# Three groups of seven products in the second pair of both down stages of a hybrid layer

## The chip, the cores and the metric

The kernel runs on 1 core of one Trainium2 chip. The metric is the device time of one execution in microseconds (us). The kernel before took 1831.77, 1834.62 and 1834.78 us in three runs, a median of 1834.62 us.

## The reference

The reference is one layer on 256 rows of width 2048, in float32. The inner width of each SwiGLU is 5632. Only the lines that bear on the change are shown:

```python
def swiglu(h, w_gate, w_up, w_down):
    return (jax.nn.silu(h @ w_gate) * (h @ w_up)) @ w_down
...
#  x += 1/2 * SwiGLU(RMSNorm(x))                 FFN1
#  h = RMSNorm(x);  [u | q | k | v] = h @ w_in
#  y_ssm = GLU(S5(u)),  y_sb = StickBreakingAttention(QKNorm(q), QKNorm(k), v)
#  x += concat(RMSNorm(y_ssm), RMSNorm(y_sb)) @ w_out
#  x += 1/2 * SwiGLU(RMSNorm(x))                 FFN2
#  x += RMSNorm((p @ w_ple_proj) * sigmoid(RMSNorm(x) @ w_ple_gate))
```

The weights of the two SwiGLU blocks are by far the largest inputs: two times three matrices of 2048 by 5632.

## The kernel before

**Products in three parts.** TensorE (PE) multiplies in a rounded float32 form (fp32r). To keep float32 accuracy every operand is split into a high and a low part: ACT casts the high part (L181), DVE subtracts it from the source for the low part (L184). A product is then three matmuls: high by high (L322, L494), activation low by weight high (L323, L495) and activation high by weight low (L327, L497). Weights arrive as `raw`, 1 MB blocks of 512 rows by 512 columns, by loads on SP's queue (L312 in columns, L511 in groups), with five buffers. Each half of such a block is split into a pair of tiles, `whi` and `wlo`, or `shi` and `slo`; where groups of seven run, `weight_pair` hands out seven such pairs in turn. Activations of a SwiGLU's inner width are split one block of 512 rows at a time (`act`, tiles `hhi` and `hlo`).

**Columns and groups of seven.** In the down stages two neighbouring column blocks of 512 (the two sides, a pair) are computed together, over eleven row blocks of the down weight, numbered 0 to 10. For one row block the program has two ways. `column(side, kb)` is the plain product, for one side: two halves of twelve matmuls, so 48 matmuls for both sides. `chunk(kb)` is a group of seven products for both sides, after Strassen's scheme as Winograd wrote it: 42 matmuls. The group takes its weights from two loads, builds three sums of them on DVE (`sum`, L501) and one by a DMA that adds in place, issued on POOL (`raw<-raw`, L525), and splits all seven operands. It needs sums of the activation's quarters too (`sum_forms`: four small DVE operations on `rows`, L458, and a split into `nhi` and `nlo`). PE takes the products of a group in the order 1, 5, 6, 4, 2, 3, 7.

**The plan of a down stage.** `plans` lists for the first and the second pair of columns what is done in which order: c is a column block for both sides, s a group of seven, a the rest of the blocks. A down stage has two pairs here, since the output has four blocks of 512 columns. `kept` holds the split of one row block, so that both sides of a column share it. After the last group, `opened` gathers finished banks into the residual `x` by seven operations of DVE (L674, L680, L685); it is put off to run beside the work that follows. While the second pair begins, the finished columns of the first pair are turned and fetched back for the next stage: `h<-mid`, small DMAs on SP (L229), and their normed split (`nhi`, `nlo`, L191 and L193).

**FFN2's first block.** The gate and up product of FFN2 goes over eleven blocks of 512 columns of the inner width. For each the program mixes groups and columns, with gate and up as the two sides and the row blocks 0 to 3 of the weight. The first block alone is done by `gemm_pair`, by columns only.

**Other places of the change.** At the start of the projection `w_in` the S5 mixer loads a table in eight pieces (`m<-scr_h`, `load_m3`, L1053, on SP); `u_block` (L1015) casts a finished block of u into `sg`, and `ua<-ub` (L1032, SP) moves it. `add_square` (L1327, L1328) squares a block on ACT into `sqp`, and POOL adds it up.

All engines execute in program order. A waiting instruction holds all that stands behind it on its engine; DMAs that SP issues stand in SP's own queue.

Of the kernel before, what the change touches and what calls it, by code (L numbers as in the profile page):

```python
# [16 lines left out]
P = 128  # L17
# [9 lines left out]
NB = 512  # L27
SL = 4
# [5 lines left out]
def layer_kernel(ctx: ExitStack, tc: tile.TileContext, a: dict, shapes: dict, out: bass.AP):  # L34
    nc = tc.nc
# [307 lines left out]
    def gemm_pair(act, ws, nkt):  # L343


        ps = [[acc(), acc()] for _ in ws]
        last = nkt // 4 - 1
        for ks in (range(last - 1), (last - 1,), (last,)):
            for (w, n0), banks in zip(ws, ps):
                for k in ks:  # L350
                    part = act(k)
                    for half in list(weight_halves(w, 4 * k, 4, n0)):
                        gemm_half(banks, (part, half), range(TT), k + half[0] == 0, k == last and half[0] == 1)
                        step()
                if last in ks:
                    yield banks
# [198 lines left out]
    def ffn(i, xn, nxt, bg=None):  # L555
# [23 lines left out]
        for f in range(NF):  # L579
            if prep and f == early:  # L580
                finish(prep)
                side.close()
                prep = None
                sevens = pools.enter_context(sums_phase(f"sums{i}"))
                hp = pools.enter_context(phase(f"h{i}b"))
                sums = [sum_forms(sevens, whole_rows(sevens, xn(kb)), "h") for kb in range(2)]
            if sevens and f:
                sg, hh = com("sg"), com("h")
                gate_cols, up_cols = ([u[:, t * NB : (t + 1) * NB] for t in range(TT)] for u in (sg, hh))

# [13 lines left out]

                s = Seven(xn, lambda kb: sums[kb], ((wg, f * NB), (wu, f * NB)), sevens)
                two = f != early
                if f == early:
                    s.column(0, (1, 2, 3))
                    s.chunk(0, (*shared, 2, 4))
                    put_off(0, opened, s)  # L610
                elif two:
                    s.chunk(0)
                    s.column(0, (2, 3))
                    s.chunk(1, (*shared, 2, 4))
                    put_off(0, opened, s)
                else:
                    s.chunk(0, shared)
                    put_off(0, opened, s)
                    s.column(0, (1, 2, 3), True)
                put_off(0, gated, s)  # L620
                s.column(1, (2, 3) if two and f != early else (1, 2, 3), True)
                nc.vector.tensor_tensor(out=hh, in0=s.banks[3.8], in1=hh, op=ALU.add)
                for t in range(TT):
                    nc.vector.scalar_tensor_tensor(
                        out=up_cols[t], in0=up_cols[t], scalar=xn.rs(t), in1=gate_cols[t], op0=ALU.mult, op1=ALU.mult
                    )
                put_off(2, turned, hp, f, hh)
                continue

            def gate():  # L630
                for t in range(TT):
# [3 lines left out]
            if f == 0 and bg:  # L635
                warm_up(10)
                first = first_quarters(wg, xn)
            if f == 0 and not bg:
                both = gemm_pair(xn, ((wg, 0), (wu, 0)), KD)
                pg = next(both)  # L640
                sums = [sum_forms(sevens, whole_rows(sevens, xn(kb))) for kb in range(2)]
            else:
                pg = gemm_block(xn, wg, f * NB, KD, first)
            sg = com("sg")
            if f == 0 and bg:
# [6 lines left out]
            pu = gemm_block(xn, wu, f * NB, KD) if f or bg else next(both)  # L652
# [23 lines left out]
        def opened(s, n):  # L676
# [10 lines left out]
            gather(xt[1][n + 1], one, -0.5)  # L687

        plans = (
            ("c3", "c4", "s0", "c5", "c6", "s1", "c7", "c8", "s2", "c9", "c10"),  # L690
            ("c2", "c3", "s0", "c4", "s1", "a5"),
        )
        for n in range(0, ND, 2):
            parts = {}

            def kept(kb):
                if kb not in parts:
                    parts.clear()
                    parts[kb] = act(kb)
                return parts[kb]  # L700
# [7 lines left out]
            s = Seven(kept, lambda kb: sum_forms(sevens, rows(kb)), ((wd, n * NB), (wd, (n + 1) * NB)), sevens)  # L708
            plan = plans[n // 2]
            left = sum(u[0] == "s" for u in plan)  # L710
            for u in plan:
                kb, final = int(u[1:]), u == plan[-1]
                if u[0] == "s":
# [320 lines left out]
    def s5_main(pool, zpool):  # L1034
# [15 lines left out]
        def load_m3(z):  # L1050
            for g in range(2):
                p0 = 64 * g + HC * z
                nc.sync.dma_start(m3[p0 : p0 + HC, :, HC * z :], scr_h[g, :, :, : (SL - z) * HC])  # L1053

# [267 lines left out]
    def add_square(pool, total, src, first):  # L1322
        if first:
            nc.scalar.activation(total, src, AF.Square)
        else:
            sq = get(pool, "sqp", T, 2)
            nc.scalar.activation(sq, src, AF.Square)  # L1327
            nc.gpsimd.tensor_tensor(out=total, in0=total, in1=sq, op=ALU.add)  # L1328

# [345 lines left out]
```

## Time and profile before

| | |
|---|---|
| runs, us | 1831.77, 1834.62, 1834.78; median 1834.62 |
| the profiled execution, us | 1829.94 |
| its span, us | 1828.1 |
| PE busy, matmuls | 1817.1 us (99%), 8960 in the trace |
| DVE busy, instructions | 1523.8 us (83%), 1789 |
| ACT busy, instructions | 1056.1 us (58%), 1228 |
| granted TensorE clock | 1.00 |
| loads of the down weights | 88 of 1024 KB, median 5.2 us from issue to landing |

The span is the part of the profiled execution that the trace covers. Busy time counts an engine's own instructions; a matmul's row (0.39 us) lasts longer than the distance to the next row's start (0.23), so rows of matmuls overlap. A row of a timeline gives the start, the length, the engine, the line, the operation and its tiles; "x4" means four in a row, and the brackets say how long the engine was idle before it and what ended that. FFN1's down stage lies at about 500 to 705 us and its second pair begins near 594.6; FFN2's second pair begins near 1603.

### The profile page before, as it was taken

Reading aid. Unit: us, or ns where it says so; the run is one execution under the profiler, and the core shown is the slowest. Engines: PE = TensorE matmul, PEld = TensorE weight load, DVE = VectorE, ACT = ScalarE, POOL = GpSimd, SP = SyncE. Lnnn points to the kernel's source line nnn. Section 1 sums busy time; section 2 is a strip of 40 time slices with the busy share of each in tenths; the row PEclk is TensorE's granted clock in tenths of the full one; section 3 lists DMA queues with packets and bytes.
Section 4 is the critical chain, followed back from the end, with each engine's and each line's share of the span. In section 5 each row is a group of like instructions: output and inputs, shape, how many; then the busy total and the mean of one; then the engine's idle time right before and its main releaser. Section 6 shows DMA issues by size and latency. Waiting matters only on the chain.

```text
span 1828.1 us, 24219 instructions
## 1 busy us (share of the span) xinstructions
PE 1817.1 (99%) x8960; PEld 1504.4 (82%) x8960; DVE 1523.8 (83%) x1789; ACT 1056.1 (58%) x1228; POOL 96.7 (5%) x147
## 2 busy tenths in 40 slices
PE   9999999999999999999999999999999999999998
PEld 7888888888888888788897888888888888888887
DVE  8966759999899895687566789999999998989565
ACT  7444445556566664455685466555565556666554
POOL 0010000000000000010021000000000010000000
PEclk9999999999999999999999999999999999999999
DMA  9898867787777676675636787887777786767563
GB/s 329 281 290 279 246 224 231 235 248 220 251 244 240 185 253 198 208 254 162 219 134 212 225 301 215 252 256 251 237 225 237 240 273 227 238 206 246 176 217 127
DMA packets 237207, 424.74 MB, mean 232 GB/s; under 512 B 27328, under 2 KB 51264, under 8 KB 236928
## 3 DMA queue, kind: packets, MB, share of 16 engines
q1 hardware_dynamic: 227104, 390.71, 64.2%
q0 software_dynamic: 9264, 31.07, 7.8%
q8 instruction: 70, 1.15, 0.3%
q10 hardware_dynamic: 720, 1.41, 0.2%
q14 instruction: 49, 0.40, 0.1%
HBM read 372.41 MB, written 10.88 MB: 210 GB/s over the span
## 4 chain that ended last, share of the span: by engine, by line
PE 98%; DMA 1%; ACT 1%; DVE 0%; SPq 0%; issue 0%; ACTq 0%; DVEq 0%
PE acc L322 18%; PE acc L323 18%; PE acc L327 18%; PE aux L327 6%; PE aux L323 6%; PE aux L322 6%; PE acc L497 4%; PE acc L495 4%; PE acc L494 4%; PE aux L495 3%; PE aux L494 3%; PE aux L497 3%; PE aux L1135 0%; PE acc L1391 0%; PE acc L1386 0%; PE acc L1382 0%
## 5 line engine op out<-in xcount | busy, mean ns | idle before, releaser
L184 DVE TENSOR_TENSOR wlo<-raw,whi 128x1024 fp32r<-128x1024 f32 x489 | 592.2, 1224 | 179.9 <-ACT whi L181 178.8
L181 ACT CAST whi<-raw 128x1024 fp32r<-128x1024 f32 x489 | 508.1, 1050 | 362.8 <-PE acc L323 227.2
L322 PE MATMUL acc<-whi,nhi 128*128 128x512 f32 x1076 | 421.9, 392 | 4.7 <-ACT whi L181 4.3
L323 PE MATMUL acc<-whi,nlo 128*128 128x512 f32 x1076 | 419.0, 389 | 0.0
L327 PE MATMUL acc<-wlo,nhi 128*128 128x512 f32 x1076 | 294.9, 389 | 0.0
L322 PEld LDWEIGHTS acc<-whi,nhi 128*128 128x128 f32 x1076 | 202.1, 188 | 49.5 <-ACT whi L181 5.9
L327 PEld LDWEIGHTS acc<-wlo,nhi 128*128 128x128 f32 x1076 | 202.0, 188 | 42.1
L323 PEld LDWEIGHTS acc<-whi,nlo 128*128 128x128 f32 x1076 | 202.0, 188 | 41.0
L184 DVE TENSOR_TENSOR slo<-raw,shi 128x1024 fp32r<-128x1024 f32 x177 | 216.1, 1221 | 21.9 <-ACT shi L181 21.5
L181 ACT CAST shi<-raw 128x1024 fp32r<-128x1024 f32 x177 | 185.8, 1050 | 61.0 <-DMA raw<-in_ffn_w_down 26.3
L181 ACT CAST whi<-sum 128x1024 fp32r<-128x1024 f32 x69 | 72.7, 1053 | 137.5 <-DVE sum L501 125.5
L181 ACT CAST shi<-sum 128x1024 fp32r<-128x1024 f32 x48 | 50.6, 1054 | 83.4 <-DVE sum L501 81.3
L501 DVE TENSOR_TENSOR sum<-sum,raw 128x1024 f32<-128x1024 f32 x78 | 95.3, 1222 | 0.5
L184 DVE TENSOR_TENSOR wlo<-sum,whi 128x1024 fp32r<-128x1024 f32 x69 | 84.5, 1224 | 5.7 <-ACT whi L181 4.7
L525 POOL DMA_DIRECT2D raw<-raw x39 | 33.7, 865 | 954.6 <-DVE sum L501 575.2
L184 DVE TENSOR_TENSOR hlo<-hT,hhi 128x1024 fp32r<-128x1024 f32 x56 | 68.3, 1220 | 4.9 <-ACT hhi L181 4.9
L323 PE MATMUL acc<-whi,hlo 128*128 128x512 f32 x184 | 71.9, 391 | 0.1
L322 PE MATMUL acc<-whi,hhi 128*128 128x512 f32 x184 | 71.6, 389 | 0.0
L181 ACT CAST hhi<-hT 128x1024 fp32r<-128x1024 f32 x56 | 58.5, 1046 | 7.3 <-PE aux L327 5.2
L322 PE MATMUL aux<-whi,hhi 128*128 128x512 f32 x160 | 62.2, 389 | 0.0
L323 PE MATMUL aux<-whi,hlo 128*128 128x512 f32 x160 | 62.2, 389 | 0.0
L184 DVE TENSOR_TENSOR slo<-sum,shi 128x1024 fp32r<-128x1024 f32 x48 | 58.7, 1223 | 1.0 <-ACT shi L181 0.7
(373 smaller groups left out, 3164.6 us busy)
## 6 DMA issues: line engine op xcount, KB each, us to landing
raw<-in_ffn_w_up SPq DMA_DIRECT2D x88, 1024.0 KB, 5.6
raw<-in_ffn_w_down SPq DMA_DIRECT2D x88, 1024.0 KB, 5.2
raw<-in_ffn_w_gate SPq DMA_DIRECT2D x86, 1024.0 KB, 7.4
raw<-in_w_in SPq DMA_DIRECT2D x32, 1024.0 KB, 5.9
raw<-raw POOLq DMA_DIRECT2D x39, 512.0 KB, 6.2
raw<-in_w_out SPq DMA_DIRECT2D x16, 1024.0 KB, 5.1
raw<-in_w_ple_gate SPq DMA_DIRECT2D x16, 1024.0 KB, 5.3
hT<-mid SPq DMA_DIRECT2D x160, 64.0 KB, 4.1
```

Of the source, the lines that this page charges most:

```text
L181: copy = nc.scalar.copy(hi, src)
L184: nc.vector.tensor_tensor(out=lo, in0=src, in1=hi.bitcast(F32), op=ALU.subtract)
L322: nc.tensor.matmul(ps[t], lhsT=lh, rhs=hi[:, j, cols], start=start and j == 0, stop=False)
L323: nc.tensor.matmul(ps[t], lhsT=ll, rhs=hi[:, j, cols], start=False, stop=False)
L327: nc.tensor.matmul(ps[t], lhsT=lh, rhs=lo[:, j, cols], start=False, stop=stop and j == 1)
L494: nc.tensor.matmul(ps, lhsT=lh[j], rhs=hi[:, j], start=begin and j == 0, stop=False)
L495: nc.tensor.matmul(ps, lhsT=ll[j], rhs=hi[:, j], start=False, stop=False)
L497: nc.tensor.matmul(ps, lhsT=lh[j], rhs=lo[:, j], start=False, stop=z in final and j == 1)
L501: nc.vector.tensor_tensor(out=t, in0=x, in1=y, op=ALU.add)
L525: nc.gpsimd.dma_start(b12, b22, accum_op=ALU.add)
```

## The change

It has four parts. The second pair of both down stages has a new plan: c10 and c9, then the groups of blocks 2, 1 and 0 one after the other, then columns 3 to 8, where the second side runs them backwards. `kept` now keeps two splits, and across the two pairs, so that blocks 9 and 10 (split last by the first pair) and block 8 at the turn of the sides are not split again; `summed` keeps the rows' sums of blocks 1 and 2 for the second pair. The first block of FFN2 gets one group of seven, for row block 0. The eight pieces of the S5 table are loaded through POOL's queue. `sqp` has six buffers instead of two.

```diff
@@ ffn: gate and up @@
-            if sevens and f:
+            if sevens:
...
-                two = f != early
-                if f == early:
+                if f == 0:
+                    sums = [sum_forms(sevens, whole_rows(sevens, xn(0)))]
+                    s.column(0, (1,))
+                    s.column(1, (1,))
+                    s.chunk(0, shared)
+                    put_off(0, opened, s)
+                    s.column(0, (2,))
+                    s.column(1, (2,))
+                    s.column(0, (3,), True)
+                    sums.append(sum_forms(sevens, whole_rows(sevens, xn(1))))
+                elif f == early:
...
-                s.column(1, (2, 3) if two and f != early else (1, 2, 3), True)
+                s.column(1, (3,) if f == 0 else (1, 2, 3) if f == early else (2, 3), True)
...
-            if f == 0 and not bg:
-                both = gemm_pair(xn, ((wg, 0), (wu, 0)), KD)
-                pg = next(both)
-                sums = [sum_forms(sevens, whole_rows(sevens, xn(kb))) for kb in range(2)]
-            else:
-                pg = gemm_block(xn, wg, f * NB, KD, first)
+            pg = gemm_block(xn, wg, f * NB, KD, first)
@@ ffn: down @@
-            ("c2", "c3", "s0", "c4", "s1", "a5"),
+            (("c", 10), ("c", 9), ("s", 2), ("s", 1), ("s", 0), ("a", (3, 4, 5, 6, 7, 8))),
...
+        parts, forms = {}, {}
+
+        def kept(kb):
+            if kb not in parts:
+                if len(parts) == 2:
+                    del parts[next(iter(parts))]
+                parts[kb] = act(kb)
+            return parts[kb]
+
+        def summed(kb):
+            if kb not in forms:
+                forms[kb] = sum_forms(sevens, rows(kb))
+            return forms.pop(kb) if kb == 0 or n else forms[kb]
+
         for n in range(0, ND, 2):
-            parts = {}
...
-                    s.column(side, (kb,) if u[0] == "c" else range(kb, F // P // 4), final)
+                    s.column(side, (kb,) if kind == "c" else kb[:: 1 - 2 * side], final)
@@ load_m3 @@
-                nc.sync.dma_start(m3[p0 : p0 + HC, :, HC * z :], scr_h[g, :, :, : (SL - z) * HC])
+                nc.gpsimd.dma_start(m3[p0 : p0 + HC, :, HC * z :], scr_h[g, :, :, : (SL - z) * HC])
@@ add_square @@
-            sq = get(pool, "sqp", T, 2)
+            sq = get(pool, "sqp", T, 6)
```

The lines behind the edits move by up to seven: L1015 becomes L1022, L1032 becomes L1039, L1045 becomes L1052.

**DVE in the second pair of FFN1's down stage.** Before, from the last splits of the group of block 0 to the first sum of the group of block 1. `raw_5358` and `raw_5406` are the two loads of column block 4 between them:

```order
L184 TENSOR_TENSOR wlo_5323<-raw_5235,whi_5322 128x1024
L184 TENSOR_TENSOR wlo_5341<-raw_5235,whi_5340 128x1024
L184 TENSOR_TENSOR hlo_5355<-hT_410_2586,hhi_5354 128x1024
L184 TENSOR_TENSOR slo_5361<-raw_5358,shi_5360 128x1024
L184 TENSOR_TENSOR wlo_5365<-raw_5358,whi_5364 128x1024
L184 TENSOR_TENSOR slo_5409<-raw_5406,shi_5408 128x1024
L184 TENSOR_TENSOR wlo_5413<-raw_5406,whi_5412 128x1024
L193 SCALAR_TENSOR_TENSOR nlo_5429<-h_5134,gains,nhi_5428 128x256 x4
L184 TENSOR_TENSOR hlo_5455<-hT_157_1040,hhi_5454 128x1024
L184 TENSOR_TENSOR nlo_5464<-rows_5458,nhi_5463 128x1024
L501 TENSOR_TENSOR sum_5467<-raw_5450,raw_5452 128x1024
L184 TENSOR_TENSOR slo_5471<-raw_5450,shi_5470 128x1024
```

Now, from the last splits of the group of block 1 to the second split of the group of block 0 (`hlo_5451` is the activation of block 0, the `rows` and `nlo_5460` are its sums of quarters, and `hlo_5541` belongs to the column that follows):

```order
L184 TENSOR_TENSOR wlo_5417<-raw_5339,whi_5416 128x1024
L193 SCALAR_TENSOR_TENSOR nlo_5427<-h_5130,gains,nhi_5426 128x256 x2
L184 TENSOR_TENSOR wlo_5437<-raw_5339,whi_5436 128x1024
L184 TENSOR_TENSOR hlo_5451<-hT_157_1040,hhi_5450 128x1024
L458 TENSOR_TENSOR rows_5454<-hT_157_1040 128x256 x2
L458 TENSOR_TENSOR rows_5454<-rows_5454,hT_157_1040 128x256
L501 TENSOR_TENSOR sum_5463<-raw_5446,raw_5448 128x1024
L458 TENSOR_TENSOR rows_5454<-hT_157_1040,rows_5454 128x256
L184 TENSOR_TENSOR slo_5467<-raw_5446,shi_5466 128x1024
L184 TENSOR_TENSOR wlo_5477<-sum_5463,whi_5476 128x1024
L184 TENSOR_TENSOR nlo_5460<-rows_5454,nhi_5459 128x1024
L184 TENSOR_TENSOR hlo_5541<-hT_282_1808,hhi_5540 128x1024
```

Before, the four splits and one activation split of block 4 stood between two groups; now the next group's activation, sums and splits follow at once, and the sums of the rows stand ahead of them. In all, the order has 126 sums L501 in place of 117, 783 splits become 792, and the activation splits `hlo` fall from 56 to 48.

**SP at the same place.** `raw_5233` and `raw_5235` are the two loads of the first group of the pair before; the `h` rows are the fetches for the next stage:

```order
L511 DMA raw_5235<-in_ffn_w_down 128x4x512
L229 DMA h_5096<-mid_5095 32x2x128 x8
L229 DMA h_5134<-mid_5095 32x2x128 x4
L229 DMA h_5096<-mid_5095 32x2x128 x4
L229 DMA h_5134<-mid_5095 32x2x128 x8
L312 DMA raw_5358<-in_ffn_w_down 128x4x512
L229 DMA h_5134<-mid_5095 32x2x128 x4
L312 DMA raw_5406<-in_ffn_w_down 128x4x512
L511 DMA raw_5450<-in_ffn_w_down 128x4x512
L511 DMA raw_5452<-in_ffn_w_down 128x4x512
```

Now, where `raw_5337` and `raw_5339` are the two loads of the group of block 1, and `raw_5446` and `raw_5448` those of block 0:

```order
L511 DMA raw_5227<-in_ffn_w_down 128x4x512
L229 DMA h_5092<-mid_5091 32x2x128 x8
L229 DMA h_5130<-mid_5091 32x2x128 x4
L229 DMA h_5092<-mid_5091 32x2x128 x4
L229 DMA h_5130<-mid_5091 32x2x128 x8
L511 DMA raw_5337<-in_ffn_w_down 128x4x512
L229 DMA h_5130<-mid_5091 32x2x128
L511 DMA raw_5339<-in_ffn_w_down 128x4x512
L229 DMA h_5130<-mid_5091 32x2x128 x3
L511 DMA raw_5446<-in_ffn_w_down 128x4x512
L511 DMA raw_5448<-in_ffn_w_down 128x4x512
```

The 24 fetches ahead are the same as before; behind them stood the loads of column block 4, one per side, and now stand both loads of the second group, with one fetch between them.

**ACT at the start of `w_in`.** Before, around the cast of the first block of u (`sg`, L1015), where `raw_6257` and `raw_6294` are weight loads of `w_in`:

```order
L181 CAST whi_6216<-raw_6214 128x1024
L191 ACTIVATE nhi_6137<-aux_6128,gains 128x256 x4
L181 CAST whi_6220<-raw_6214 128x1024
L1015 ACTIVATE sg_6252<-acc_6056,sm_6192 128x512
L1015 ACTIVATE sg_6252<-acc_6057,sm_6192 128x512
L181 CAST whi_6259<-raw_6257 128x1024
L181 CAST whi_6263<-raw_6257 128x1024
L181 CAST whi_6296<-raw_6294 128x1024
L181 CAST whi_6300<-raw_6294 128x1024
L181 CAST whi_6339<-raw_6337 128x1024
L181 CAST whi_6343<-raw_6337 128x1024
```

Now the same block, whose cast is L1022:

```order
L181 CAST whi_6204<-raw_6202 128x1024
L191 ACTIVATE nhi_6125<-aux_6116,gains 128x256 x4
L181 CAST whi_6208<-raw_6202 128x1024
L181 CAST whi_6247<-raw_6245 128x1024
L181 CAST whi_6251<-raw_6245 128x1024
L181 CAST whi_6284<-raw_6282 128x1024
L181 CAST whi_6288<-raw_6282 128x1024
L1022 ACTIVATE sg_6240<-acc_6044,sm_6180 128x512
L1022 ACTIVATE sg_6240<-acc_6045,sm_6180 128x512
L181 CAST whi_6327<-raw_6325 128x1024
L181 CAST whi_6331<-raw_6325 128x1024
```

Four casts of weights that stood behind the block's cast stand ahead of it. On SP, seven loads of `w_in` now stand ahead of the first `ua<-ub` instead of four, counted from the load of `raw_6159` (now `raw_6147`).

More of the change, by code (lines that the diff above doesn't have):

```diff
@@ L610, in ffn @@
                     put_off(0, opened, s)
-                elif two:
+                else:
                     s.chunk(0)
@@ L615, in ffn @@
                     put_off(0, opened, s)
-                else:
-                    s.chunk(0, shared)
-                    put_off(0, opened, s)
-                    s.column(0, (1, 2, 3), True)
                 put_off(0, gated, s)
-                s.column(1, (2, 3) if two and f != early else (1, 2, 3), True)
+                s.column(1, (3,) if f == 0 else (1, 2, 3) if f == early else (2, 3), True)
                 nc.vector.tensor_tensor(out=hh, in0=s.banks[3.8], in1=hh, op=ALU.add)
@@ L634, in ffn @@
             first = ()
-            if f == 0 and bg:
+            if f == 0:
                 warm_up(10)
                 first = first_quarters(wg, xn)
-            if f == 0 and not bg:
-                both = gemm_pair(xn, ((wg, 0), (wu, 0)), KD)
-                pg = next(both)
-                sums = [sum_forms(sevens, whole_rows(sevens, xn(kb))) for kb in range(2)]
-            else:
-                pg = gemm_block(xn, wg, f * NB, KD, first)
+            pg = gemm_block(xn, wg, f * NB, KD, first)
             sg = com("sg")
-            if f == 0 and bg:
+            if f == 0:
                 for n in range(ND):
@@ L651, in ffn @@
                 gate()
-            pu = gemm_block(xn, wu, f * NB, KD) if f or bg else next(both)
+            pu = gemm_block(xn, wu, f * NB, KD)
             if prep and f == 0:
@@ L689, in ffn @@
         plans = (
-            ("c3", "c4", "s0", "c5", "c6", "s1", "c7", "c8", "s2", "c9", "c10"),
-            ("c2", "c3", "s0", "c4", "s1", "a5"),
-        )
-        for n in range(0, ND, 2):
-            parts = {}
[L696 to L700, printed above, removed]
+            (("c", 3), ("c", 4), ("s", 0), ("c", 5), ("c", 6), ("s", 1), ("c", 7), ("c", 8), ("s", 2), ("c", 9), ("c", 10)),
+            (("c", 10), ("c", 9), ("s", 2), ("s", 1), ("s", 0), ("a", (3, 4, 5, 6, 7, 8))),
+        )
+        parts, forms = {}, {}
[9 more added lines that the diff above has]
+            return forms.pop(kb) if kb == 0 or n else forms[kb]
+        for n in range(0, ND, 2):
             def end(side):
@@ L706, in end @@
                 put_off(0 if m == ND - 1 and m < nxt.early else 2, nxt.block, m)
-            s = Seven(kept, lambda kb: sum_forms(sevens, rows(kb)), ((wd, n * NB), (wd, (n + 1) * NB)), sevens)
+            s = Seven(kept, summed, ((wd, n * NB), (wd, (n + 1) * NB)), sevens)
             plan = plans[n // 2]
[L710 to L713, printed above, removed]
+            left = sum(kind == "s" for kind, _ in plan)
+            for kind, kb in plan:
+                final = (kind, kb) == plan[-1]
+                if kind == "s":
                     left -= 1
```

## The prediction

> **What bounds the kernel now.** I read the page first (busy shares, the chain that ended last), then PE's waits, then the span in windows of 25 us, and last the timelines of single engines at the places that the change touches. The profiled execution took 1829.94 us, and its span is 1828.1.
>
> ```profile
> span 1828.1 us, 24219 instructions
> PE 1817.1 (99%) x8960; PEld 1504.4 (82%) x8960; DVE 1523.8 (83%) x1789; ACT 1056.1 (58%) x1228; POOL 96.7 (5%) x147
> PE 98%; DMA 1%; ACT 1%; DVE 0%; SPq 0%; issue 0%; ACTq 0%; DVEq 0%
> PE acc L322 <- ACT whi L181: 4.3, 4, 2.1
> ```
>
> PE (matmuls) is busy for 99% of the span, and the chain of waits lies on it. Whatever adds no PE wait costs nothing, and a matmul taken out is worth its full time. The last row, from PE's waits, is nearly all the time that PE loses: 4.3 us in four waits for a cast of ACT. DVE's 83% is a mean, and says nothing of single stages. The windows do (columns: PE, PEld, DVE, ACT, POOL busy us, PE's granted clock, DMA share, GB/s):
>
> ```profile
> 575.00:600.00 25.00, 25.00 (x112) 20.70 (x111) 23.89 (x28) 15.07 (x22) 0.00 (x0) 1.00 0.75 255
> 600.00:625.00 25.00, 25.00 (x112) 20.68 (x111) 20.77 (x24) 14.75 (x19) 0.85 (x1) 1.00 0.65 187
> 625.00:650.00 25.00, 25.00 (x112) 20.71 (x111) 24.82 (x27) 18.37 (x21) 2.67 (x2) 1.00 0.72 231
> 1000.00:1025.00 25.00, 25.00 (x112) 20.68 (x111) 21.35 (x29) 14.47 (x22) 1.09 (x2) 1.00 0.75 232
> 1025.00:1050.00 25.00, 25.00 (x112) 20.71 (x111) 17.06 (x27) 11.97 (x18) 1.08 (x2) 1.00 0.60 190
> 1400.00:1425.00 25.00, 25.00 (x112) 20.69 (x111) 24.87 (x24) 13.66 (x14) 1.71 (x2) 1.00 0.76 245
> ```
>
> The second pair of FFN1's down stage begins at about 594.6. Around its second group of seven (625 to 650), DVE is at 24.82 of 25 us while PE is still full: DVE has nothing to spare where groups of seven run. The clock is 1.00, so a matmul costs the same everywhere.
>
> **Matmuls removed.** Their rate comes from PE's rows in the middle of the kernel:
>
> ```profile
> 731.28 1.07 PE L327 MATMUL acc<-wlo,nhi 128*128 128x512 f32 x4
> 734.00 1.07 PE L327 MATMUL acc<-wlo,nhi 128*128 128x512 f32 x4
> 563.30:572.82 9.52, 9.52 (x43) 7.88 (x42) 9.52 (x11) 7.97 (x10) 0.00 (x0) 1.00 0.77 249
> ```
>
> One half of a weight block is twelve matmuls, and 2.72 us pass from one to the next, so a matmul costs 0.2267 us. The window of a whole group of seven agrees: 42 matmuls in 9.52 us. A block done as a group instead of two columns saves 48 - 42 = 6 matmuls. There is one more group in each down stage, and one in the first column block of FFN2: 18 matmuls, 18 x 0.2267 = **4.1 us gained**.
>
> **Three groups in a row: DVE's account.** A group costs DVE seven weight splits and three sums (L501), all 128x1024, and PE 9.52 us. DVE's rate:
>
> ```profile
> 594.78 1.29 DVE L674 SCALAR_TENSOR_TENSOR x<-aux,x 128x512 f32<-128x512 f32 x2 [0.59 <-PE aux L327]
> 602.48 1.22 DVE L184 TENSOR_TENSOR slo<-raw,shi 128x1024 fp32r<-128x1024 f32 x1
> 603.62 1.22 DVE L501 TENSOR_TENSOR sum<-sum,raw 128x1024 f32<-128x1024 f32 x1
> 616.37 0.43 DVE L458 TENSOR_TENSOR rows<-hT 128x256 f32<-128x256 f32 x1
> 616.71 0.42 DVE L458 TENSOR_TENSOR rows<-hT,rows 128x256 f32<-128x256 f32 x1
> 617.04 2.36 DVE L184 TENSOR_TENSOR wlo<-raw,whi 128x1024 fp32r<-128x1024 f32 x2
> 626.66 1.67 DVE L193 SCALAR_TENSOR_TENSOR nlo<-h,gains,nhi 128x256 fp32r<-128x256 f32 x4
> 628.25 1.22 DVE L184 TENSOR_TENSOR hlo<-hT,hhi 128x1024 fp32r<-128x1024 f32 x1
> ```
>
> Wide operations start 1.14 us apart (602.48, 603.62), small rows 0.34 (616.37, 616.71), four nlo take 1.59 (626.66 to 628.25). The ten wide ones of a group are then 11.4 us of DVE against 9.52 of PE, before its activation split (1.14) and row sums. Columns of one block give 10.9 us of PE for four splits and at most one hlo, 5.7 us. Groups of seven need columns between them to be paid for; the new plan has none between s2, s1 and s0.
>
> In the changed kernel c10 and c9 come first, 96 matmuls, from 594.6 to 616.4. The three groups, 126 matmuls or 28.6 us, would end at 644.9 without a stall. DVE can't prepare the groups ahead: the ring holds seven weight pairs, so the seventh split of s2 needs a pair that the last half of c9 frees at 616.4. I put that split at 617.0, where its like stands today (617.04). From there DVE has, in the order listed in the part on the change: that split; for s1 seven splits, three sums and hlo; for s0 the same eleven and nlo from the rows; and hlo of the next column: 1 + 11 + 12 + 1 = 25 wide operations, 25 x 1.137 = 28.4 us. To these come 1.6 (four nlo), 1.4 (four rows) and 0.6 (one gather): 32.0 us. The last two matmuls of s0 (0.45) follow the last split, so the groups end at 617.0 + 32.0 + 0.45 = 649.5, which is **4.6 us** late.
>
> Three more terms. First the loads of s1:
>
> ```profile
> 596.13 17.91 SPq L229 DMA_DIRECT2D h<-mid  x24
> 614.14 0.53 SPq L312 DMA_DIRECT2D raw<-in_ffn_w_down  x1
> 617.32 0.53 SPq L312 DMA_DIRECT2D raw<-in_ffn_w_down  x1
> 620.03 1.05 ACT L181 CAST shi<-raw 128x1024 fp32r<-128x1024 f32 x1 [1.89 <-DMA raw<-in_ffn_w_down]
> 623.09 1.06 ACT L181 CAST shi<-raw 128x1024 fp32r<-128x1024 f32 x1 [0.65 <-DMA raw<-in_ffn_w_down]
> 1622.79 0.53 SPq L312 DMA_DIRECT2D raw<-in_ffn_w_down  x1
> ```
>
> Twenty-four small fetches of the next stage's rows hold SP for 17.9 us. A weight load behind them is issued at 614.14 and used at 620.03, 5.9 us later; the next one takes 5.8 (617.32 to 623.09). In the changed kernel both loads of s1 stand there: the first at 614.1, the second one fetch later, at about 615.3. Its first sum reads both. DVE is ready at 617.0 + 2 x 1.14 = 619.3, and what stands behind the sum on DVE is the whole of s1, with PE waiting for it. At the earliest the wait is nothing (SP faster than today), at the latest 3.7 us (the two loads share the engines and land at 623.0); 5.9 us after 615.3 is 621.2, plus some sharing 621.8: I take 2.5. The second down stage has the same fetches and the same load behind them (1622.79), so it is counted alike. [...]
>
> Second, the order within a group (in s1 the split that product 4 needs stands behind that of product 2, in s0 product 5 waits for the nlo of the rows): between 0 and 1.3 us, of which I take 0.3, since in today's windows such waits end before PE needs the pair. Third, the seven gathers after s0 stand among c3's splits: 0 to 0.9 us, taken at 0.6, since PE has no lead left there. The eight hlo splits and two row sums that the reuse removes lie in the columns, where DVE has time: nothing, and the three more splits of the groups are counted above.
>
> One stage: 4.6 + 2.5 + 0.3 + 0.6 = **8.0 us lost** (bounds 4.6 and 10.5), two stages **16.0**.
>
> **FFN2's first block.** The group stands alone among columns. It adds three sums, and seven splits stand for four: 6 x 1.14 = 6.8 us of DVE. From 1000 to 1050, where this block runs, DVE has 50 - 21.35 - 17.06 = 11.6 us to spare. I take nothing; if the work fell in the first window alone, with its 3.65 us, 3.2 would be lost.
>
> **The eight m loads go to POOL.** SP, ACT and PE today:
>
> ```profile
> 708.47 9.10 SPq L1053 DMA_DIRECT2D m<-scr_h  x8
> 736.93 5.00 SPq L1032 DMA_DIRECT2D ua<-ub  x8
> 742.03 1.67 SPq L312 DMA_DIRECT2D raw<-in_w_in  x3
> 734.88 1.27 ACT L1015 ACTIVATE sg<-acc,sm 128x512 f32<-128x512 f32 x2 [10.51 <-PE acc L327]
> 736.03 3.88 ACT L181 CAST whi<-raw 128x1024 fp32r<-128x1024 f32 x4
> 747.86 2.00 ACT L181 CAST whi<-raw 128x1024 fp32r<-128x1024 f32 x2 [7.94 <-DMA raw<-in_w_in]
> 737.13 0.50 PE L322 MATMUL acc<-whi,nhi 128*128 128x512 f32 x1 [2.06 <-ACT whi L181]
> 748.96 0.50 PE L322 MATMUL acc<-whi,nhi 128*128 128x512 f32 x1 [0.64 <-ACT whi L181]
> ```
>
> PE loses 2.06 us because four casts stand on ACT behind sg, which waits for PE's block to end, and 0.64 because three loads stand on SP behind ua. Each m load holds SP for 1.1 us. In the new order the four casts stand ahead of sg, and all these loads ahead of ua: **2.7 us gained**, at worst nothing. [...]
>
> **Six sqp buffers.** Today:
>
> ```profile
> 965.44 0.39 ACT L1327 ACTIVATE sqp<-aux 128x256 f32<-128x256 f32 x1 [1.08 <-POOL sqa L1328]
> 966.26 0.38 ACT L1327 ACTIVATE sqp<-aux 128x256 f32<-128x256 f32 x1 [0.43 <-POOL sqa L1328]
> 970.08 0.47 PE L322 MATMUL acc<-whi,nhi 128*128 128x512 f32 x1 [1.14 <-ACT whi L181]
> ```
>
> ACT waits 1.08 + 0.43 us for POOL to free a buffer; a cast stands behind, and PE waits 1.14 for it. With the buffers the casts come 1.5 us earlier: **1.1 us gained**, at worst nothing.
>
> **The sum.** Gains 4.1 + 2.7 + 1.1 = 7.9; losses 16.0; net 8.1 us more: 1838.0 against 1829.94 of the profiled execution. The median of the runs stands 4.7 above that execution, so I forecast **1842.7**. With 4.6 per stage it is 1835.9, with 10.5 and neither of the last two gains 1851.5. A measurement here tells 0.2%, 3.7 us, from no change.
>
> **Rivals.**
> *The lead hides it (faster).* The seven pairs in flight cover more than I count: DVE enters s2 with everything but one split done and the loads of s1 land by 619. For it: at 1400 to 1425 DVE is at 24.87 of 25 and PE has no wait. Against it: there columns stand between the groups. It decides below a stall of 7.9 / 2 = 3.95 us per stage; at 2.0 the time is 1834.6 + 4.0 - 7.9 = 1830.7, without a stall 1826.7.
> *Only DVE's deficit remains (no change).* SP issues the fetches faster and the loads cost nothing, the ends are smoothed: 4.6 per stage, 9.2 - 7.9, 1835.9. For it: SP's 0.75 us per fetch is a rate of this place. Against it: both down stages show it.
> *Everything adds (slower still).* Full load wait, 10.5 per stage: 1834.6 + 21.0 - 7.9 = 1847.7. For it: with PE at DVE's pace, nothing catches up until the columns. Against it: the bounds would all have to be met.
> *The m loads bring nothing (slower).* ACT's casts wait for loads or pairs where they now wait for sg, and the 2.7 us stay: 1845.4. [...] That the m loads become late themselves I leave out: they are first read at 754.6, and were issued from 708.47.
>
> ```profile
> L1080 PE MATMUL aux<-ua,m x256: 218/218/267, 754.6 to 832.4; 64*64 64x64 f32 x128
> ```
>
> **How the numbers follow.** My forecast 0.46, the lead 0.18, deficit only 0.13, everything adds 0.13, m loads 0.10. Faster 0.18, within 0.2% 0.13, slower 0.69. My forecast's own range is 1836 to 1851; down to 1831 it takes in half of the faster case, and above 1851 I leave out little.
>
> **What would show it.** Right: PE waits for DVE's slo or wlo in the products of s1 and s0, about 625 to 655 and the like near 1630 to 1660, with DVE busy throughout but for one wait on raw near 619; PE's waits near 737, 749 and 970 gone; 8942 matmul rows in place of 8960. Wrong: no PE wait in those groups, or a DVE that idles there for another cause, or the waits at 737 and 970 still there.

## The result, and the profile after

The changed kernel took a median of 1847.0 us (1843.89 to 1848.25, six runs) against 1832.83 us before (1831.77 to 1834.78, six runs). The ratio is 1.0077, with a 95% interval of 1.0066 to 1.0088: slower, by some 14 us. The forecast was slower by 8.1 us.

The page of the changed kernel's profiled execution (1847.42 us), its busy times and its chain of waits:

```profile
span 1845.6 us, 24183 instructions
PE 1824.4 (99%) x8942; PEld 1506.0 (82%) x8942; DVE 1535.6 (83%) x1795; ACT 1054.9 (57%) x1228; POOL 103.4 (6%) x158
PE 89%; DVE 5%; DMA 3%; issue 1%; SPq 1%; ACT 1%; DVEq 0%; ACTq 0%; POOLq 0%
```

Eighteen matmuls are gone (8942 for 8960), yet PE is busy 7.3 us longer. Their rows last longer in places: 0.63 us at 646.70, where the granted clock is 0.50 (both below), in place of 0.39. The chain of waits has left PE for 11% of the span, DVE being the largest part.

The windows of 25 us in which PE is not full (columns as before: PE, PEld, DVE, ACT, POOL, PE's granted clock, DMA share, GB/s):

```profile
625.00:650.00 25.00, 20.81 (x71) 14.95 (x70) 25.00 (x29) 16.48 (x19) 1.13 (x2) 0.81 0.50 128
700.00:725.00 25.00, 24.15 (x107) 19.66 (x106) 13.46 (x16) 9.97 (x13) 5.01 (x10) 1.00 0.73 232
1350.00:1375.00 25.00, 22.14 (x91) 17.48 (x90) 19.38 (x20) 13.56 (x16) 0.87 (x1) 0.93 0.65 198
1625.00:1650.00 25.00, 24.30 (x108) 19.80 (x106) 19.24 (x21) 16.56 (x23) 0.86 (x1) 1.00 0.58 171
1650.00:1675.00 25.00, 20.28 (x74) 14.99 (x73) 24.63 (x30) 14.46 (x16) 0.86 (x1) 0.86 0.61 193
```

A full window holds 112 matmuls. From 625 to 650 there are 71: 41 x 0.2267 = 9.3 us lost in FFN1's second pair. From 1625 to 1675 there are 42 too few, 9.5 us, in FFN2's. From 1350 to 1375 there are 21 too few, 4.8 us, in FFN2's gate and up stage. From 700 to 725 five, 1.1 us. Together 24.7; less the forecast gains of 7.9 that is 16.8 of the 17.5 us by which the span grew.

DVE and PE in FFN1's groups of blocks 1 and 0:

```profile
622.17 1.22 DVE L501 TENSOR_TENSOR sum<-raw,raw 128x1024 f32<-128x1024 f32 x1 [2.08 <-DMA raw<-in_ffn_w_down]
649.55 2.35 DVE L184 TENSOR_TENSOR wlo<-raw,whi 128x1024 fp32r<-128x1024 f32 x2
```

```profile
640.00 0.76 PE L497 MATMUL acc<-slo,hhi 128*128 128x512 f32 x2 [2.03 <-DVE slo L184]
642.27 0.79 PE L495 MATMUL acc<-whi,nlo 128*128 128x512 f32 x1 [0.87 <-DVE nlo L184]
645.67 0.80 PE L494 MATMUL aux<-shi,nhi 128*128 128x512 f32 x1 [0.90 <-ACT shi L181]
646.70 0.63 PE L494 MATMUL aux<-shi,nhi 128*128 128x512 f32 x1
647.12 0.63 PE L495 MATMUL aux<-shi,nlo 128*128 128x512 f32 x1
654.99 0.39 PE L322 MATMUL acc<-shi,hhi 128*128 128x512 f32 x1
```

DVE waits 2.08 us for the loads of s1, then runs without a gap, and its last split of s0 ends at 651.9. PE waits for it several times. But at 646.70 nothing is waited for, and the next matmul starts 0.42 us later instead of 0.23. The first matmul of the columns stands at 654.99. That is 10.1 us behind the 644.9 of the prediction, but here the pair began 0.5 us later: the first group starts at 616.86, and its 126 x 0.2267 us would end at 645.4, so the loss is 9.6 us. FFN2's second pair, from 1634.73 to 1672.87, gives 9.6 by the same sum. The same place in windows of 2 us shows why:

```profile
640.00:642.00 2.00, 1.40 (x3) 0.58 (x3) 2.00 (x2) 1.15 (x2) 0.00 (x1) 0.64 0.84 154
648.00:650.00 2.00, 2.00 (x6) 1.61 (x5) 2.00 (x3) 2.00 (x3) 0.24 (x1) 0.50 0.30 13
650.00:652.00 2.00, 2.00 (x8) 1.60 (x8) 2.00 (x3) 1.31 (x2) 1.57 (x1) 0.80 0.85 323
```

The granted clock falls to 0.50 at about 640.6 (0.64 over two us is 0.50 for 72% of them) and is back at about 650.8. PE takes some 10 us at half speed when it should be catching up.

### The profile page after: what moved, and what is told of

The parts are those of the page before. It is cut to its first block, busy times and chain, and to the rows that moved or that the text cites. A ratio compares the mean times of both kernels' runs of the same rounds, so it can differ in the third digit from the quotient of the medians.

```text
span 1845.6 us, 24183 instructions
## 1 busy us (share of the span) xinstructions
PE 1824.4 (99%) x8942; PEld 1506.0 (82%) x8942; DVE 1535.6 (83%) x1795; ACT 1054.9 (57%) x1228; POOL 103.4 (6%) x158
## 4 chain that ended last, share of the span: by engine, by line
PE 89%; DVE 5%; DMA 3%; issue 1%; SPq 1%; ACT 1%; DVEq 0%; ACTq 0%; POOLq 0%
PE acc L322 17%; PE acc L323 17%; PE acc L327 17%; PE aux L323 5%; PE aux L327 5%; PE aux L322 5%; PE acc L494 3%; PE acc L497 3%; PE acc L495 3%; PE aux L494 3%; PE aux L497 3%; PE aux L495 3%; DVE wlo L184 1%; DVE slo L184 1%; DMA h<-mid 1%
## 5 line engine op out<-in xcount | busy, mean ns | idle before, releaser
L322 PE MATMUL acc<-whi,nhi 128*128 128x512 f32 x1052 | 412.6, 392 | 1.0 <-ACT whi L181 0.4
L323 PE MATMUL acc<-whi,nlo 128*128 128x512 f32 x1052 | 409.6, 389 | 0.0
L327 PE MATMUL acc<-wlo,nhi 128*128 128x512 f32 x1052 | 288.9, 389 | 0.0
L181 ACT CAST shi<-sum 128x1024 fp32r<-128x1024 f32 x56 | 58.9, 1052 | 88.7 <-DVE sum L501 81.4
L501 DVE TENSOR_TENSOR sum<-sum,raw 128x1024 f32<-128x1024 f32 x84 | 102.5, 1220 | 0.6
L184 DVE TENSOR_TENSOR slo<-sum,shi 128x1024 fp32r<-128x1024 f32 x56 | 68.4, 1221 | 2.5 <-ACT shi L181 2.0
L501 DVE TENSOR_TENSOR sum<-raw,raw 128x1024 f32<-128x1024 f32 x42 | 51.2, 1220 | 11.8 <-DMA raw<-in_ffn_w_down 10.6
L322 PE MATMUL aux<-whi,nhi 128*128 128x512 f32 x156 | 60.7, 389 | 0.0
L323 PE MATMUL aux<-whi,nlo 128*128 128x512 f32 x156 | 60.7, 389 | 0.0
L181 ACT CAST hhi<-hT 128x1024 fp32r<-128x1024 f32 x48 | 50.2, 1047 | 17.9 <-PE acc L327 9.7
```

What stands on the lines that cost most here:

```text
L181: copy = nc.scalar.copy(hi, src)
L184: nc.vector.tensor_tensor(out=lo, in0=src, in1=hi.bitcast(F32), op=ALU.subtract)
L322: nc.tensor.matmul(ps[t], lhsT=lh, rhs=hi[:, j, cols], start=start and j == 0, stop=False)
L323: nc.tensor.matmul(ps[t], lhsT=ll, rhs=hi[:, j, cols], start=False, stop=False)
L327: nc.tensor.matmul(ps[t], lhsT=lh, rhs=lo[:, j, cols], start=False, stop=stop and j == 1)
L501: nc.vector.tensor_tensor(out=t, in0=x, in1=y, op=ALU.add)
```

## The experiments

All times are medians beside runs of the kernel before on the same chip; ratios are to that kernel, with 95% intervals.

| run | us | before, us | ratio |
|---|---|---|---|
| e1_old_plan | 1828.43 | 1831.68 | 0.9983 (0.9973 to 0.9992) |
| e2_spread | 1832.64 | 1831.68 | 1.0009 (0.9999 to 1.0018) |
| e4_no_sums | 1829.40 | 1831.68 | 0.9990 (0.9981 to 1.0000) |
| e5_more_matmuls | 1848.30 | 1831.68 | 1.0092 (1.0077 to 1.0107) |
| e3_fetch_on_pool | 1839.50 | 1831.57 | 1.0044 (1.0031 to 1.0058) |
| e6_old_plan_m_on_sp | 1832.59 | 1831.57 | 1.0006 (0.9997 to 1.0014) |
| e8_old_first_block | 1828.09 | 1831.57 | 0.9978 (0.9970 to 0.9987) |
| e9_spread_fetch_on_pool | 1839.72 | 1831.57 | 1.0047 (1.0033 to 1.0061) |
| e7_old_plan_two_sqp | 1831.11 | 1831.63 | 0.9998 (0.9989 to 1.0007) |
| e12_plan_alone | 1849.56 | 1831.63 | 1.0093 (1.0079 to 1.0106) |
| e11_spread_sum_on_pool | 1838.71 | 1831.63 | 1.0044 (1.0027 to 1.0061) |

**The old plan in the changed kernel, and the new plan in the old kernel.**

```diff
-            (("c", 10), ("c", 9), ("s", 2), ("s", 1), ("s", 0), ("a", (3, 4, 5, 6, 7, 8))),
+            (("c", 2), ("c", 3), ("s", 0), ("c", 4), ("s", 1), ("a", (5, 6, 7, 8, 9, 10))),
```

> The changed kernel with the old plan of the second pair (two groups, c2 c3 s0 c4 s1 and columns 5 to 10); the other parts stay. Theory A: all of the loss is the new plan's. Left are 6 matmuls fewer (1.4 us), the waits near 737 and 749 (2.7) and the one near 970 (1.1): 5.2 us under before, about 1827.6, with no PE wait in the second pairs and a clock of 1.00 there. Rival B: another part (FFN2's first block, the kept splits) costs a good part, as the 4.8 us lost near 1355 in the changed kernel's profile might say: 1831 to 1836, with PE waits in FFN2's gate and up stage.

Measured 1828.43, 3.2 us under the kernel before, where the forecast for A was 5.2. No PE wait is left in the second pairs; near 1345 PE waits 1.3 us (1.08 and 0.26), which A did not foresee and e8_old_first_block settles below. The other way round, the kernel before with the plan and its reuse alone (the edits to FFN2's first block, `load_m3` and `add_square` undone):

> The kernel before with only the new plan of the second pairs and its reuse of splits and sums (FFN2's first block by columns, m loads on SP, two sqp buffers). Theory A: 12 matmuls fewer, 2.7 us, and 10.1 + 8.7 us lost in the second pairs as in the changed kernel's profile: 16.1 over before, about 1847.7, with the half clock in both pairs or one; no PE wait near 1350. Rival: the loss in the second pairs owes part to the other parts of the change: 1842 or less.

Measured 1849.56, 17.9 over the kernel before by the medians (17.0 by the ratio) against 16.1 expected. Its windows of the two second pairs:

```profile
625.00:650.00 25.00, 19.78 (x71) 14.28 (x70) 25.00 (x29) 16.63 (x19) 1.08 (x2) 0.86 0.49 128
1625.00:1650.00 25.00, 25.00 (x111) 20.57 (x110) 20.19 (x22) 16.72 (x22) 0.88 (x1) 1.00 0.65 182
1650.00:1675.00 25.00, 20.49 (x69) 15.05 (x69) 23.73 (x27) 15.58 (x17) 0.87 (x1) 0.80 0.59 182
```

The same 71 matmuls, and 44 too few in FFN2's: the loss comes with the plan alone. PE loses some more in waits that the other parts take away (3.08 us at 757 and 1.14 at 981), and from 1350 to 1375 it is full here.

**Is it DVE's account?** The three sums of a group are left out in the second pairs:

```diff
         def add(self, x, y):
+            if self.light:
+                return x
...
+            s.light = n > 0
             plan = plans[n // 2]
```

> The changed kernel without the three sums of each group in the second pairs (a product that takes a sum of weight quarters takes the first quarter instead): nine wide DVE operations less in a stage, 10.2 us. Theory A (DVE's account sets the loss): 10.2 is more than DVE is late (about 7 us in each second pair), so PE's waits in s1 and s0 vanish and the clock stays at 1.00: 1828 to 1831. Rival C (the late weight loads of s1 set it): the loads are as late as before, PE still waits 2 to 4 us in each stage and the clock still falls: 1838 or more.

Measured 1829.40, 16 us (by the ratios) to 17.6 (by the medians) under the changed kernel, with nine of DVE's wide operations less per stage. The windows 625 to 650 and 1645 to 1670 hold 112 matmuls each at a clock of 1.00. Rival C fell. Behind the groups PE still waits for hlo (0.41 us at 656.6, 1.13 at 1674.9), and without any loss the forecast gains alone would have given 1823.8. Leaving out a sum also spares the cast that waits for it, so this run alone does not tell DVE's time from that chain; in the changed kernel it is told by DVE, which works without a gap from 622.17 to the last split.

**More work for PE in the same place** (`more` is set in the second pairs).

```diff
             for j in range(2):
+                if self.more:
+                    nc.tensor.matmul(ps, lhsT=ll[j], rhs=lo[:, j], start=False, stop=False)
                 nc.tensor.matmul(ps, lhsT=lh[j], rhs=lo[:, j], start=False, stop=z in final and j == 1)
```

> The changed kernel with two matmuls more in each product of the second pair's groups (activation low by weight low): 42 a stage, 84 in all, 19.0 us of PE work at 0.2267. Theory A with the clock: the groups end when DVE ends (about 652 in the profile) and PE's waits and the half clock behind them (some 10 us a stage) are what the work fills: 1847 within 3 us, clock 1.00 in 625 to 660. Rival D: the waits are for single operations and the work adds to them: 1856 to 1866.

Measured 1848.30: by the ratios 0.15% (2.7 us) over the changed kernel, for 84 matmuls or 19.0 us of work. The windows:

```profile
625.00:650.00 25.00, 24.80 (x107) 19.61 (x106) 24.96 (x28) 15.75 (x18) 1.50 (x3) 1.00 0.49 129
1650.00:1675.00 25.00, 24.15 (x104) 19.03 (x103) 24.97 (x29) 14.13 (x16) 0.86 (x1) 1.00 0.65 199
```

PE now does 107 matmuls where it did 71, DVE is as full as before, and the clock is 1.00. In FFN1 the last split of s0 ends at 651.7 as before (651.9), and the columns begin at 656.0 in place of 655.0, though PE has 9.5 us more to do in the groups: what it does while it would wait, or work at half speed, is nearly free. D fell. In this run the end is PE's own: it has 4.3 us of matmuls left when DVE is done, and it hardly waits.

**The loads behind the fetches.** The fetches of the first pair's rows are issued on POOL:

```diff
-                put_off(0 if m == ND - 1 and m < nxt.early else 2, nxt.block, m)
+                put_off(0 if m == ND - 1 and m < nxt.early else 2, nxt.block, m, *(() if n else (nc.gpsimd,)))
...
-    def turn_quarters(out, mid, steps):
+    def turn_quarters(out, mid, steps, queue=nc.sync):
```

> The changed kernel with the fetches of the first pair's rows (h<-mid, 32 in each down stage) issued on POOL in place of SP, so that no weight load stands behind them. Theory A: DVE's waits for s1's loads (2.1 and 2.7 us) go, DVE and the groups end that much earlier, and a shorter PE wait may spare the half clock too: 4 to 9 us under the changed kernel, 1838 to 1843. Rival: POOL holds the adding DMA of the groups behind the fetches, and product 7 waits for it: 1847 or more.

Measured 1839.50, 7.5 us under the changed kernel by the medians, 6.0 by the ratios. DVE no longer waits for s1's loads; the largest PE wait in FFN1's second pair that stays is

```profile
644.74 0.79 PE L494 MATMUL aux<-shi,nhi 128*128 128x512 f32 x1 [1.97 <-ACT shi L181]
```

and the half clock behind it lasts 3.4 us instead of 10. In FFN2's second pair the clock does not fall at all. By the windows, counted in matmuls as above, the two pairs lose 5.7 us less than in the changed kernel's profile, against 2.1 and 2.7 us of waits for the loads; the rest goes with the half clock, 3.4 us in place of 10.2 in FFN1 and none in place of 6.8 in FFN2; that the shorter PE wait spared it was not tried by itself. The profiles differ by 3.2 us more from 1350 to 1375, where this one has 105 matmuls in place of 91; those belong to the wait near 1355, which the part on FFN2's first block takes up.

**Three groups, spread.** Another plan, then the same plan with the fetches on POOL, then with one sum of each group on POOL:

```diff
-            (("c", 10), ("c", 9), ("s", 2), ("s", 1), ("s", 0), ("a", (3, 4, 5, 6, 7, 8))),
+            (("s", 2), ("c", 10), ("s", 1), ("c", 9), ("s", 0), ("a", (3, 4, 5, 6, 7, 8))),
```

> The changed kernel with its three groups spread (s2 c10 s1 c9 s0 and columns 3 to 8): as many groups, matmuls and sums, with columns of one block behind each group. Theory A: the groups cost only because they stand in a row; about 7.9 us under before, 1825, PE waits in the second pairs under 1 us each. Rival: three groups in a pair are too much for DVE wherever they stand, and half of the loss stays: 1834 or more.

Measured 1832.64: the clock stays at 1.00, and of the 14 us most is gone, but the 7.9 us that were to be won on top are not there. PE still waits for splits in both pairs:

```profile
642.55 0.50 PE L494 MATMUL acc<-whi,hhi 128*128 128x512 f32 x1 [1.43 <-ACT whi L181]
```

These waits are 5.5 us in the two stages, with one of 0.76 at the end of the first. The idle time is not all that a wait took: the row of PE ahead of it lasts 0.39 us, and where nothing is waited for the next row starts 0.23 us after it. Counted in matmuls, the windows from 625 to 675 and from 1625 to 1675 hold 99, 108, 104 and 102, which is 35 too few or 7.9 us: the whole of the gain.

> The spread plan (e2_spread, 1832.6, PE waits of some 5.5 us in the two second pairs) with the fetches on POOL. Theory: DVE's wait for the loads of s1 (2.3 us near 609 in e2_spread) is what leaves DVE late later on; without it the waits fall to 1 to 2 us in all: 1827 to 1829, below e1_old_plan or equal to it. Rival: DVE is short of time there anyway: 1831 to 1833.

Measured 1839.72, 7 us worse than without the move, and outside of both the theory and the rival. DVE's wait for the loads of s1 is gone, but PE waits for casts near 618, 624 and 1633 (1.13, 1.98 and 1.48 us). In this run ACT and DVE stand waiting for the fetched rows, ahead of the sums and casts of s1:

```profile
611.08 1.31 ACT L191 ACTIVATE nhi<-h,gains 128x256 fp32r<-128x256 f32 x3 [7.10 <-DMA h<-mid]
611.62 0.89 DVE L193 SCALAR_TENSOR_TENSOR nlo<-h,gains,nhi 128x256 fp32r<-128x256 f32 x2 [5.26 <-ACT nhi L191]
```

The first sum of s1 starts at 615.29; in e2_spread it started at 609.76, with the rows' splits behind it. What helped in one order hurt in the other.

For the last run, `other` is set in the second pairs:

```diff
-            t1 = self.add(b11, b12)
+            t1 = self.add(b11, b12, nc.gpsimd if self.other else nc.vector)
```

> The spread plan (e2_spread, 1832.6) with the first of the three weight sums of each group in the second pairs made on POOL in place of DVE: 3.4 us less of DVE in a stage. Theory A: the waits left in e2_spread (some 5.5 us in both second pairs) are DVE's shortness, and most go: 1827 to 1829. Rival: POOL makes the sum so much slower (a 128x256 add took it 0.9 to 1.1 us, so some 4 for this size, an estimate) that product 5 or the sums behind it wait: 1833 or more.

Measured 1838.71: the rival. The sums on POOL:

```profile
L502 POOL TENSOR_TENSOR sum<-raw,raw 128x1024 f32<-128x1024 f32 x6 | 16.9, 2809 | 142.6 <-DMA raw<-in_ffn_w_down 78.0 <-DMA h<-mid 46.2 <-DVE wlo L184 18.4
```

A sum takes 2.81 us in the mean in place of DVE's 1.22, at the head of a chain of casts and further sums. PE's waits in the two pairs grow from 4.7 us to 8.8, and from 1656.0 the clock is at 0.50 for 6.8 us.

**The smaller parts, in the kernel with the old plan.**

```diff
-                nc.gpsimd.dma_start(m3[p0 : p0 + HC, :, HC * z :], scr_h[g, :, :, : (SL - z) * HC])
+                nc.sync.dma_start(m3[p0 : p0 + HC, :, HC * z :], scr_h[g, :, :, : (SL - z) * HC])
```

> The kernel with the old plan (e1_old_plan, 1828.4), with the eight m loads back on SP. As predicted: PE's waits near 737 and 749 come back, 2.7 us: 1831.1. Rival, that an issuing engine matters little: 1828.4, no such waits.

Measured 1832.59. By the ratios that is 0.23%, 4.2 us, over e1_old_plan. Its profile has the two waits again:

```profile
737.79 0.50 PE L322 MATMUL acc<-whi,nhi 128*128 128x512 f32 x1 [2.06 <-ACT whi L181]
749.53 0.50 PE L322 MATMUL acc<-whi,nhi 128*128 128x512 f32 x1 [0.57 <-ACT whi L181]
```

They are 2.6 of the 4.2 us. Another 1.8 us are waits for hlo near 658 and 1672 that e1_old_plan's profile does not have; e7_old_plan_two_sqp and e8_old_first_block, where the m loads are on POOL, have such waits too (1.01, 0.86 and 1.45 us), so they are not the m loads' doing.

```diff
-            sq = get(pool, "sqp", T, 6)
+            sq = get(pool, "sqp", T, 2)
```

> The kernel with the old plan (e1_old_plan, 1828.4), with two sqp buffers again. As predicted: PE's wait near 970 comes back, 1.1 us: 1829.5. Rival: ACT's waits for POOL were hidden, or the order moves so that the wait does not come back: 1828.4.

Measured 1831.11, 0.15% or 2.7 us over e1_old_plan. The wait is back, 1.14 us as it was before; the profiled execution also lost 3.2 us near 660, by two waits and a half clock behind them:

```profile
970.88 0.47 PE L322 MATMUL acc<-whi,nhi 128*128 128x512 f32 x1 [1.14 <-ACT whi L181]
658.44 0.50 PE L322 MATMUL acc<-whi,hhi 128*128 128x512 f32 x1 [0.51 <-ACT hhi L181]
659.95 0.50 PE L323 MATMUL acc<-whi,hlo 128*128 128x512 f32 x1 [1.01 <-DVE hlo L184]
```

**FFN2's first block and the wait near 1355.** ACT's rows there, first before and then in the changed kernel:

```profile
1344.47 1.05 ACT L181 CAST whi<-sum 128x1024 fp32r<-128x1024 f32 x1 [1.45 <-DVE sum L501]
1348.84 1.05 ACT L181 CAST whi<-raw 128x1024 fp32r<-128x1024 f32 x1 [2.37 <-DMA raw<-raw]
```

```profile
1345.70 1.05 ACT L181 CAST whi<-sum 128x1024 fp32r<-128x1024 f32 x1 [0.19 <-DVE sum L501]
1354.72 1.04 ACT L181 CAST shi<-raw 128x1024 fp32r<-128x1024 f32 x1 [7.97 <-DMA raw<-raw]
1355.67 1.04 ACT L181 CAST whi<-sum 128x1024 fp32r<-128x1024 f32 x1
```

Before, the cast that waits for the adding DMA stood behind the casts of the sums. Now it stands ahead of the last of them, and all of ACT's casts wait with it. To undo the new group in FFN2's first block:

```diff
-            if sevens:
+            if sevens and f:
...
-            pg = gemm_block(xn, wg, f * NB, KD, first)
+            if f == 0 and not bg:
+                both = gemm_pair(xn, ((wg, 0), (wu, 0)), KD)
+                pg = next(both)
+                sums = [sum_forms(sevens, whole_rows(sevens, xn(kb))) for kb in range(2)]
+            else:
+                pg = gemm_block(xn, wg, f * NB, KD, first)
...
```

> The kernel with the old plan (e1_old_plan, 1828.4), with FFN2's first block by columns only again: 6 matmuls more, 1.4 us. Theory: the group there shifts which pair of the ring each later product of the stage gets, and so ACT's order; the cast that waits for the adding DMA near 1345 then stands ahead of casts that PE needs. Without the group the waits near 1345 (1.3 us in e1_old_plan) go: 1828.4 within 1. Rival: they have to do with something else and stay: 1829.8.

Measured 1828.09, and no PE wait near 1345: as the theory had it. The other profiles agree: the three kernels with the first block by columns (before, this one and e12_plan_alone) have no PE wait there, and all ten with the group have one. That the ring's phase is the way by which the group changes ACT's order was argued from the rows (whi in one, shi in the other) and not tried by itself.

e1_old_plan and e8_old_first_block are both faster than either kernel: 0.9983 and 0.9978 of the time before. They keep the moved loads and the six buffers, and the two groups of the old plan.

## Why the prediction was right or wrong

**Right: the sign and what decides it.** DVE's account of the three groups set the end. The forecast had its last split end at 617.0 + 32.0 + 2.5 = 651.5; it ended at 651.9. The wait for s1's loads was forecast as 2.5 us and measured 2.08 and 2.73. e4_no_sums removed DVE's work and with it nearly all of the loss, e5_more_matmuls added PE's work and added nearly nothing.

**Too small: the loss of a stage.** The forecast was 8.0 us, the profile shows 9.6 in each. The step that failed is the first part's "The clock is 1.00, so a matmul costs the same everywhere". That held for the kernel before, whose granted clock was 1.00. The last split of s0 being ready at 651.9, PE could have ended near 652.4 and ended at 654.99: 2.6 us, because it worked at half speed from 640.6 to 650.8 and still had products to do. In FFN2 the last split of s0 ends at 1670.4 and the columns begin at 1672.87, 2.0 us later than they could, with half speed until 1668.0. DVE's own part came out near the forecast, 6.9 us in FFN1 and 7.6 in FFN2 where 4.6 and 2.5 were counted, so what was missing is a term for the clock. The 0.6 us for the gathers were not lost: PE waits nowhere in the columns behind s0. Behind the stalls that I counted as so many us of DVE, PE worked at a clock of 0.50 for 10.24 us in FFN1 and 6.83 in FFN2.

**Not foreseen: FFN2's gate and up stage.** Of the first block the prediction said "I take nothing". DVE is indeed not short there, but the group moved ACT's order some 300 us later, which cost 4.8 us in the profiled execution, of which 2.86 are a wait and the rest half clock (0.50 for 3.41 us). In the other runs with the new first block PE waits 0.3 to 1.3 us at the same place, so the size changes from one profile to the next; the first block brings nothing on balance (e8_old_first_block against e1_old_plan).

**Not foreseen, small:** a wait for hlo at 710, 0.85 us; each kernel with three groups has one near 700 to 710, e1_old_plan and e8_old_first_block have none.

**The gains.** The 18 matmuls are gone. The waits near 737, 749 and 970 are gone in the changed kernel, and come back with 2.6 and 1.14 us in e6_old_plan_m_on_sp and e7_old_plan_two_sqp, as forecast; the medians moved by 4.2 and 2.7, so part of each is something else. That the 18 matmuls are worth 4.1 us no run shows by itself: e1_old_plan has six fewer than e8_old_first_block and is no faster, having the wait near 1345. The rival that moving the m loads brings nothing fell: on SP they bring the waits back, and with them ACT's order, the four casts behind sg.

**The rivals.** The lead of seven pairs did not hide it. "Everything adds" (1847.7) came nearest in its number, and not by its mechanism: the load wait was not 3.7 us.

## What to carry to other kernels

Where one engine prepares what PE consumes, compare the two per block and count the blocks in a row: a group that saves PE 1.4 us and costs the other engine more than PE's own time needs cheaper blocks behind it. Price a PE stall with its tail: in the changed kernel 3.41 to 10.24 us at a clock of 0.50 stood behind three of them. And look at the order of the engines far from an edit: a group added in one block moved a wait some 300 us behind it.

## What the runs showed of the hardware that was not expected

The granted clock fell to 0.50 after short stalls and stayed there for 3.4 us or two or three times that: in the changed kernel for 10.24, 3.41 and 6.83 us, from 640.57, 1357.37 and 1661.15. The changed kernel's windows around 1357:

```profile
1356.00:1358.00 2.00, 1.24 (x4) 0.78 (x4) 2.00 (x2) 2.00 (x3) 0.00 (x0) 0.84 0.08 33
1358.00:1360.00 2.00, 2.00 (x5) 1.50 (x5) 2.00 (x3) 2.00 (x4) 0.00 (x0) 0.50 0.00 0
1360.00:1362.00 2.00, 2.00 (x8) 1.59 (x7) 2.00 (x3) 2.00 (x4) 0.00 (x0) 0.81 0.65 136
```

Half speed holds for 32% of the first, all of the second and 38% of the third window, 3.4 us; from 640.6 to 650.8 it is 10.2, three times that. In this profile the times at 1.00 between the falls, 706.56 and 300.37 us, are whole multiples of 3.413 us too, 207 and 88 of them. What stood ahead of a fall is not one length of wait: 2.06 us at 737 left the clock at 1.00 before the change, and behind 0.51 + 1.01 us between 657.9 and 660.0 in e7_old_plan_two_sqp it fell to 0.50.

The two differ in PE's idle time, taken in pieces of 3.413 us. The following are such pieces: two of the changed kernel and two of e7_old_plan_two_sqp, ahead of a fall and behind it, and two of the kernel before, around its wait of 2.06 us (they meet at 736.01, 320 pieces ahead of 1828.27, where its clock falls behind the program's end):

```profile
1353.95:1357.37 3.42, 0.61 (x3) 0.52 (x4) 1.58 (x2) 2.65 (x3) 0.00 (x0) 1.00 0.31 113
1357.37:1360.78 3.41, 3.41 (x9) 2.35 (x8) 3.41 (x4) 3.41 (x5) 0.00 (x0) 0.50 0.12 8
```

```profile
657.14:660.55 3.41, 1.90 (x8) 1.03 (x7) 3.41 (x4) 2.19 (x3) 0.00 (x0) 1.00 0.78 267
660.55:663.97 3.42, 3.42 (x10) 2.68 (x9) 3.42 (x4) 2.26 (x3) 0.00 (x0) 0.50 0.58 176
```

```profile
732.59:736.01 3.42, 2.48 (x11) 1.70 (x10) 0.41 (x1) 1.13 (x2) 0.00 (x0) 1.00 0.00 0
736.01:739.42 3.41, 2.29 (x10) 1.90 (x11) 3.20 (x5) 3.41 (x5) 0.00 (x0) 1.00 0.25 38
```

The wait of 2.06 us at 737 lies across two pieces, so that PE is idle for 0.94 us in one and 1.12 in the next, and the clock stays; in e7_old_plan_two_sqp the two shorter waits lie in one piece, 1.51 us in all, and it drops. In the changed kernel the pieces ahead of the three falls hold 2.03, 2.81 and 1.94 us of PE idle (from 637.15, 1353.95 and 1657.74); the one from 1647.50 holds 1.22, and the clock stays at 1.00. At 0.50, those from 640.57, 643.98 and 1661.15 hold 0.87, 0.90 and 1.18 us, and it stays down; those from 647.39, 1357.37 and 1664.57 hold none, and it comes back. The idle times rest on modelled ends of matmuls, so they are rough. No run changed the length or the place of one wait alone: why the clock falls is not shown, only what stood ahead of it in these profiles.
